# A fused ReGLU layer: w1's first columns by plain load on ScalarE's queue, four plain column blocks, sums moved to GpSimd, rows of x in quarters, a later fit check, another exit

## The chip, the cores and the metric

The kernel runs on one core of one Trainium2 chip. The metric is the time of one execution on the device in microseconds (us), as a median of several executions. A span is the part of it that the profile sees; it is about 1.8 us shorter than the time. All executions told of here were of the fast state.

## The reference

```python
# x: 16 x 256 x 512, w1: 512 x 4096, w2: 2048 x 512, all float32
def reference(x, w1, w2):
    h = x @ w1
    gate, value = np.split(h, 2, axis=-1)
    h = np.maximum(gate, 0) * value
    return (h @ w2).astype(np.float32)
```

## The kernel before

The 4096 rows of x are worked through in four sets of 1024. Each set has a first layer (16 blocks of 128 hidden columns) and a second layer. Both multiply 2x2 blocks of half matrices in float16 by seven products instead of eight (Winograd's form of Strassen's algorithm, P1 to P7). For this, sums S1 to S4 of the left operand and T1 to T4 of the right one must be made. The second layer of one set is interleaved with the first layer of the next.

```python
SUMS = (("S1", "A21", "A22", ADD), ("S2", "S1", "A11", SUB), ("S4", "A12", "S2", SUB), ("S3", "A11", "A21", SUB))
TURNS = (("T1", "B12", "B11", SUB), ("T2", "B22", "T1", SUB), ("T3", "B22", "B12", SUB), ("T4", "B21", "T2", SUB))

def g_sum(eng, go, n, h0, h1):      # a sum of the hidden values g, for the second layer
    for m, i0, i1, op in SUMS:
        if m == n:
            eng.tensor_tensor(go[n][:, h0:h1], go[i0][:, h0:h1], go[i1][:, h0:h1], op=op)
```

At the very start nothing is summed yet, so the first NPLAIN = 2 blocks are computed plainly. The first columns of w1 come by GpSimd's loads, which turn float32 into float16 on their way:

```python
for b in (0, 2):
    nc.sync.dma_start(out=xf[:, b:b + 2], in_=x_v[0, :, b:b + 2])
fetch_w1(0, 0)                      # nc.gpsimd.dma_start into a float16 tile
make_identity(nc, ident[F32])
fetch_w1(0, 1)
# ... (the other loads; two plain blocks; VectorE makes the weight sums of blocks 2 and 3)
```

At the end of the first set's first layer VectorE makes all sums of g and the sum T4 of w2, while GpSimd has made T1 to T3 earlier:

```python
if s == 0:
    for m in ("S1", "S2", "S4", "S3"):
        for h in (0, NHC // 2):
            g_sum(nc.vector, go, m, h, h + NHC // 2)
    w2_op(nc.vector, "T4", 2)
```

A tile of output rows b of the upper half is `o1`, of the lower half `o2`. All lie in four buffers of one name. In the order of use o1(0), o1(1), o1(2), o2(0), o2(1), the fifth needs the buffer of the first, whose store must have landed:

```python
d["o1"] = tmp.tile([P, DO], F32, name="o", tag="o", bufs=4)     # P2
# ...
nc.sync.dma_start(out=out_v[s, 0, b], in_=d["o1"])              # P3
# ...
d["o2"] = tmp.tile([P, DO], F32, name="o", tag="o", bufs=4)     # P7
```

ScalarE sums squares of x, w1 and w2, to see at run time whether their scale suits the float16 way. The rows of x for that come from DRAM, half a set at a time, into one buffer (`xn`). In the last set VectorE judges the sums, TensorE counts across partitions, and VectorE writes a flag. A branch on the flag runs a general way where the scale does not fit (it does fit here):

```python
BESIDE[NS - 1, 3] = [judge]         # and, in it, count at step 5, flag at step 8
BESIDE[NS - 1, 14] = [...]          # the flag is read
# ...
with tc.If(unfit > 0):
    general_way(...)
```

Of the kernel before, what the change touches and what calls it, by code (L numbers as in the profile page):

```python
# [17 lines left out]
TH = 512  # L18
PERIOD = 7
NWARM = 7  # L20
NFILL = 8
NPLAIN = 2
HIGH, LOW = 512.0, 32.0
GS = 2.0 ** -19
SLOT = {"P1": 0, "P5": 1, "P2": 3, "P6": 4, "P3": 5, "P7": 9, "P4": 13}
# [4 lines left out]
@with_exitstack  # L30
def kernel(ctx: ExitStack, tc: tile.TileContext, x, w1, w2, out):






    nc = tc.nc
    x2 = x.flatten_outer_dims()
    out2 = out.flatten_outer_dims()  # L40
    flagpool = ctx.enter_context(tc.tile_pool(name="flagpool", bufs=1))
    flag = flagpool.tile([1, 1], dt.int32, name="flag")
    with ExitStack() as fast:
        unfit = fast_way(fast, tc, x2, w1, w2, out2, flag)
    with tc.If(unfit > 0):
        with ExitStack() as general:
            general_way(general, tc, x2, w1, w2, out2)

# [51 lines left out]
def fast_way(ctx, tc, x2, w1, w2, out2, flag):  # L100
# [23 lines left out]
    x_v = x2.rearrange("(s b p) d -> s p b d", p=P, b=2 * NB)  # L124
    out_v = out2.rearrange("(s h b p) n -> s h b p n", p=P, b=NB, h=2)

    CHUNKS = ((0, 2), (2, 2), (4, 4), (8, 4), (12, 4))
    place = {jb + i: (c, i) for c, (jb, n) in enumerate(CHUNKS) for i in range(n)}
    wr = [wpool.tile([P, 4, 2, n * P], F16, name=f"wr{c}") for c, (_, n) in enumerate(CHUNKS)]
    wt = [wpool.tile([P, 4, 2, n * P], F16, name=f"wt{c}") for c, (_, n) in enumerate(CHUNKS)]  # L130
# [112 lines left out]
    class Plain:  # L243
        def __init__(self, g, jb):
            self.g, self.jb = g, jb

        def open(self):
            self.X = psx.tile([P, TH], F32, name="X", tag="X")
            self.W = psw.tile([P, TH], F32, name="W", tag="W")

        def mm(self, side, a, q):
            ts = slice(q * 256, q * 256 + 256)
            ps = (self.X, self.W)[side]
            for e in range(4):
                name = (("B11", "B21"), ("B12", "B22"))[side][e // 2]
                nc.tensor.matmul(ps[:, ts], W(name, self.jb)[:, e % 2], a[:, e, ts], start=e == 0, stop=e == 3,  # L256
                                 skip_group_check=True)
# [18 lines left out]
    def mm2_stream(s, go):  # L276
# [14 lines left out]
        def step(name, b):  # L291
# [18 lines left out]
            elif name == "P3":  # L310
                yield from mm("P3", b, d["W"], False)
                nc.vector.scalar_tensor_tensor(out=d["o1"][:, HALF:], in0=d["W"], scalar=1 / GS, in1=d["pu"][:, 1],  # L312
                                               op0=MULT, op1=ADD)
                nc.sync.dma_start(out=out_v[s, 0, b], in_=d["o1"])
            elif name == "P7":
                yield from mm("P7", b, d["Y"], False)
                d["o2"] = tmp.tile([P, DO], F32, name="o", tag="o", bufs=4)
                nc.vector.scalar_tensor_tensor(out=d["o2"][:, HALF:], in0=d["Y"], scalar=1 / GS, in1=d["pu"][:, 0],
                                               op0=MULT, op1=ADD)
                if last and b == NB - 1:  # L320
                    nc.sync.dma_start(out=out_v[s, 1, b, :, HALF:], in_=d["o2"][:, HALF:])
            else:
                yield from mm("P4", b, d["Y"], False)
                if last and b == NB - 1:
                    m = HALF // 2
                    nc.scalar.activation(d["o2"][:, :m], d["Y"][:, :m], COPY, scale=1 / GS)
                    nc.scalar.dma_start(out=out_v[s, 1, b, :, :m], in_=d["o2"][:, :m])
                    nc.vector.tensor_scalar(out=d["o2"][:, m:HALF], in0=d["Y"][:, m:], scalar1=1 / GS, scalar2=None,
                                            op0=MULT)
                    nc.sync.dma_start(out=out_v[s, 1, b, :, m:HALF], in_=d["o2"][:, m:HALF])  # L330
                else:
                    nc.scalar.activation(d["o2"][:, :HALF], d["Y"], COPY, scale=1 / GS)
                    nc.sync.dma_start(out=out_v[s, 1, b], in_=d["o2"])
# [33 lines left out]
    g, go = g_tiles()  # L367
    xf = go["S1"].rearrange("p a t -> p (a t)").bitcast(F32).rearrange("p (b d) -> p b d", b=NB)
    xh = go["S2"][:, :NB]

    def turn_first(o, h, b0):
        if h == 0:
            for b in (b0, b0 + 1):
                ps = psy.tile([P, 4, P], F32, name="Y", tag="Y")
                for e in range(4):
                    nc.tensor.transpose(ps[:, e], xf[:, b, e * P:(e + 1) * P], ident[F32])
                copy = nc.scalar.copy if b % 2 else nc.vector.tensor_copy
                copy(out=o["A1"][:, :, b * P:(b + 1) * P], in_=ps)
            return
        ps = psx.tile([P, 4, 2, P], F16, name="X", tag="X")  # L380
        for b in range(2):
            for e in range(4):
                nc.tensor.transpose(ps[:, e, b], xh[:, b0 + b, e * P:(e + 1) * P], ident[F16])
        nc.vector.tensor_copy(out=o["A2"][:, :, b0 * P:(b0 + 2) * P], in_=ps.rearrange("p e b t -> p e (b t)"))

    for b in (0, 2):
        nc.sync.dma_start(out=xf[:, b:b + 2], in_=x_v[0, :, b:b + 2])
    fetch_w1(0, 0)
    make_identity(nc, ident[F32])
    fetch_w1(0, 1)  # L390
    for b in (0, 2):
        nc.gpsimd.dma_start(out=xh[:, b:b + 2], in_=x_v[0, :, NB + b:NB + b + 2])
    make_identity(nc, ident[F16])
    for c in range(1, len(CHUNKS)):
        for g_ in range(2):
            fetch_w1(c, g_)

    xo = x_tiles()
    plain = [Plain(g, jb) for jb in range(NPLAIN)]

    def plain_mm(h, q):
        for side in range(2):
            for p in plain:
                p.mm(side, xo[f"A{h + 1}"], q)

    idle(NWARM)
    turn_first(xo, 0, 0)
    idle(NFILL)
    for p in plain:
        p.open()  # L410
    for p in plain:
        p.mm(0, xo["A1"], 0)
    turn_first(xo, 0, 2)
    for p in plain:
        p.mm(1, xo["A1"], 0)
    idle(3)
    plain_mm(0, 1)
    for p in plain:
        p.close(0)
    turn_first(xo, 1, 0)  # L420
    for p in plain:
        p.open()
    plain_mm(1, 0)
    turn_first(xo, 1, 2)
    plain_mm(1, 1)
    sums = list(SUMS)

    def x_sum(o):
        n, i0, i1, op = sums.pop(0)
        nc.vector.tensor_tensor(o[n], o[i0], o[i1], op=op)  # L430

    x_sum(xo)
    plain[0].close(1)
    x_sum(xo)
    w1_first = [t for t in TURNS]

    def w1_one():
        m, a, b, o = w1_first.pop(0)
        nc.vector.tensor_tensor(W(m, 2, 2), W(a, 2, 2), W(b, 2, 2), op=o)  # L439

    w1_one()
    plain[1].close(1)
    w1_one()
    x_sum(xo)
    w1_one()
    x_sum(xo)
    w1_one()

    def look_x(s, i):
        b = i // 2 % NB  # L450
        t = xn if s else (xf, xh)[i // 2 // NB]
        look(t[:, b, i % 2 * 256:i % 2 * 256 + 256], 4 * NB * s + i, 256)

    def look_w1(i):
        c, o = place[i // 2 * 2]
# [2 lines left out]
    def look_w2(i):  # L458
        look(w2_sb[:, 2 * i:2 * i + 2].rearrange("p h n -> p (h n)"), NW + i, 1024)

    def fetch_rows(s, h):
        t = xpool.tile([P, NB, D], F16, name="xn")
        nc.sync.dma_start(out=t, in_=x16[s][h * TH:(h + 1) * TH].rearrange("(b p) d -> p b d", p=P))
        return t

    def judge():
        n = st.shape[1]
# [4 lines left out]
        nc.vector.memset(fit, 1.0)  # L472
        with nc.allow_low_precision("whole numbers below 2048"):
            nc.vector.tensor_reduce(out=fit[:, :1], in_=ok, axis=mybir.AxisListType.X, op=ADD)
        BESIDE[NS - 1, 5] = [lambda: count(fit, P * n)]

    def count(fit, n):
        ps = psw.tile([P, TH], F32, name="W", tag="W")
        nc.tensor.matmul(ps[:1, :1], fit[:, :1], fit[:, 1:], start=True, stop=True)
        BESIDE[NS - 1, 8] = [lambda: nc.vector.tensor_scalar(out=flag, in0=ps[:1, :1], scalar1=n - 0.5, scalar2=None,  # L480
                                                             op0=LT)]

    LOOKS = {}

    for s in range(NS):
        for i in range(4 * NB):
            LOOKS[s, min(i + 2, NJ - 1) if s == 0 else i] = [lambda s=s, i=i: look_x(s, i)] + (
                LOOKS.get((s, NJ - 1), []) if s == 0 and i > NJ - 3 else [])
    for s in range(NS - 1):
        for i in range(8):  # L490
            f = (lambda i=i + 8 * s: look_w1(i)) if s < 2 else (lambda i=i: look_w2(i))
            BESIDE[s, 7 + 2 * i] = [f]
    BESIDE[NS - 1, 3] = [judge]
    verdict = []
    BESIDE[NS - 1, 14] = [lambda: verdict.append(nc.values_load(
        flag[0:1, 0:1], min_val=0, max_val=1, skip_runtime_bounds_check_because="a comparison wrote it"))]

    prev = None
# [2 lines left out]
    for s in range(NS):  # L501
# [21 lines left out]
        for at in range(first * PERIOD, last + PERIOD):  # L523
            if at in plan:
                jb, n = plan[at]
                if n == "P1" and s and jb == 4:
                    late = fetch_rows(s, 1)
                if n == "P1" and s and jb == 8:
                    xn = late
                getattr(blocks[jb], n)()  # L530
                if n == "P5":
                    for f in LOOKS.get((s, jb), ()):
# [9 lines left out]
            else:  # L542
                advance(prev, 4)
        if s == 0:
            for m in ("S1", "S2", "S4", "S3"):
                for h in (0, NHC // 2):
                    g_sum(nc.vector, go, m, h, h + NHC // 2)
            w2_op(nc.vector, "T4", 2)
        else:
            for m in ("S1", "S2", "S4"):  # L550
                g_sum(nc.vector, go, m, NHC - BY_DVE, NHC)
# [1 line left out]
        if s + 1 < NS:  # L553
            xo = x_tiles()
            for h in range(2):
                for k in range(2):
                    nc.sync.dma_start_transpose(out=xo[f"A{h + 1}{k + 1}"],
                                                in_=x16[s + 1][h * TH:(h + 1) * TH, k * 256:k * 256 + 256])
            xn = fetch_rows(s + 1, 0)
            advance(stream, 100)  # L560
            sums = list(SUMS)
            for _ in SUMS:
                x_sum(xo)
            if s == 0:
                w1_ops(nc.vector, 0, 2)
            advance(stream, MM2 - TAIL - 100 - done)
        else:
            advance(stream, MM2)
# [30 lines left out]
```

## Time and profile before

| | before |
|---|---|
| time, median of 3 | 332.25 us (330.86 to 333.29) |
| span of the profiled execution | 332.0 us (that execution took 333.9) |
| TensorE busy | 93% of the span |
| mean granted clock in it | 0.984 |
| idle time of TensorE from 8.5 to 33.7 us | 8.2 us |
| the first second layer: VectorE's first sum of g to the first product of set 1 | 23.86 us |
| last product to end of span | 5.76 us |

In a waits view each line is: engine, tile and line that waited, "<-" what it waited for, then us in total, number of waits, longest. In a timeline each line is: start, length, engine, line, operation, output "<-" inputs, shapes, number of instructions, and in brackets the idle time before them and what ended it. The lines of before are in the prediction.

### The profile page before, as it was taken

The page shows a single profiled execution, that of the slowest core. Times are in us where ns is not written, and L with a number is a line of the kernel's source. Part 1 is how long each engine was busy: PE and PEld are TensorE (multiplying, and loading weights), DVE is VectorE, ACT ScalarE, POOL GpSimd, SP SyncE. Part 2 cuts the span into 40 slices and gives each one's busy share as a digit, 9 for nine tenths or more (in the row PEclk, how much of TensorE's full clock was granted, in tenths as well). Part 3 has the DMA queues.
Part 4 walks back from the last instruction along what each step waited for, and adds up shares of the span by engine and source line. Part 5 has one row for each costly group of instructions (what it writes and reads, how often), then busy time and mean ns, then how long its engine had stood idle before and what let it go on. Part 6 is the DMA issues. An engine that isn't in the chain of part 4 may idle for free.

```text
span 332.0 us, 5158 instructions
## 1 busy us (share of the span) xinstructions
PE 309.3 (93%) x1879; PEld 184.7 (56%) x1879; DVE 217.8 (66%) x338; ACT 187.5 (56%) x449; POOL 144.3 (43%) x128
## 2 busy tenths in 40 slices
PE   8756999999799999999999999999999999997993
PEld 4632444457684443448884443458884443455882
DVE  1369888879835887886526887885527887885211
ACT  2214667657457665655856766665856666752230
POOL 8359999800001334994001334993001434993000
PEclk9998999999999999999999999999999999998997
DMA  8999996036311010017311010017321020000113
GB/s 192 200 207 207 200 198 131 0 65 126 126 65 63 3 32 31 1 21 167 133 69 61 0 52 13 0 33 148 141 89 38 2 63 0 1 2 0 65 67 131
DMA packets 29390, 26.07 MB, mean 79 GB/s; under 512 B 13648, under 2 KB 24784, under 8 KB 29264
## 3 DMA queue, kind: packets, MB, share of 16 engines
q0 software_dynamic: 8080, 9.96, 17.7%
q1 hardware_dynamic: 21136, 15.67, 15.8%
q8 instruction: 16, 0.26, 0.3%
q14 instruction: 14, 0.11, 0.1%
q10 hardware_dynamic: 144, 0.07, 0.1%
HBM read 24.12 MB, written 11.53 MB: 107 GB/s over the span
## 4 chain that ended last, share of the span: by engine, by line
PE 81%; DVE 11%; ACT 2%; issue 2%; DMA 2%; DVEq 0%; ACTq 0%
PE Y L203 22%; PE X L203 14%; PE W L203 14%; PE Y L283 11%; PE W L283 8%; PE X L283 6%; DVE g_S L272 3%; PE Y L175 2%; DVE x_S L430 1%; DVE wt L439 1%; DVE cc L230 1%; DMA xn<-x 1%; PE X L256 1%; DVE g L240 1%; DVE cc L236 1%
## 5 line engine op out<-in xcount | busy, mean ns | idle before, releaser
L272 POOL TENSOR_TENSOR g_S<-g 128x512 f16<-128x512 f16 x42 | 48.5, 1154 | 144.0 <-DVE g L240 144.0
L203 PEld LDWEIGHTS <-wt 128*128 128x128 f16 x496 | 48.3, 98 | 68.3 <-issue 9.8
L203 PE MATMUL Y<-x_S,wt 128*128 128x512 f16 x248 | 74.2, 381 | 1.1 <-DVE x_S L430 1.0
L203 PE MATMUL X<-x_A,wr 128*128 128x512 f16 x248 | 74.1, 380 | 0.0
L230 DVE SCALAR_TENSOR_TENSOR cc<-W,pu 128x512 f32<-128x512 f32 x62 | 42.8, 691 | 39.4 <-ACT pu L224 36.4
L203 PEld LDWEIGHTS <-wr 128*128 128x128 f16 x372 | 36.3, 98 | 43.5 <-issue 2.6
L210 ACT COPY Y<-X 128x512 f32<-128x512 f32 x62 | 35.4, 571 | 42.0 <-PE X L203 26.9
L283 PEld LDWEIGHTS <-g_S 128*128 128x128 f16 x512 | 50.4, 99 | 7.9 <-DVE g_S L272 1.6
L224 ACT ACTIVATE pu<-Y 128x512 f32<-128x512 f32 x62 | 36.9, 596 | 15.7 <-PE Y L203 15.7
L231 DVE SCALAR_TENSOR_TENSOR g<-X,cc 128x512 f16<-128x512 f32 x62 | 42.9, 691 | 2.4
L240 DVE SCALAR_TENSOR_TENSOR g<-Y,cc 128x512 f16<-128x512 f32 x62 | 42.2, 681 | 2.8 <-PE Y L203 2.8
L283 PEld LDWEIGHTS <-g 128*128 128x128 f16 x384 | 37.8, 99 | 10.5 <-issue 2.0
L236 DVE SCALAR_TENSOR_TENSOR cc<-Y,pu 128x512 f32<-128x512 f32 x62 | 42.2, 681 | 0.3
L203 PE MATMUL Y<-x_A,wt 128*128 128x512 f16 x124 | 36.7, 377 | 4.0 <-DVE cc L236 4.0
L203 PE MATMUL W<-x_S,wt 128*128 128x512 f16 x124 | 37.2, 382 | 3.1 <-DVE wt L439 3.1
L217 ACT ACTIVATE pu<-W 128x512 f32<-128x512 f32 x62 | 37.4, 602 | 3.3 <-PE W L203 3.3
L203 PE MATMUL W<-x_S,wr 128*128 128x512 f16 x124 | 37.1, 381 | 0.3 <-DVE x_S L430 0.3
L283 PE MATMUL X<-w_sb,g 128*128 128x256 f16 x256 | 32.2, 277 | 0.0
L312 DVE SCALAR_TENSOR_TENSOR o<-W,pv 128x256 f32<-128x256 f32 x16 | 6.7, 423 | 38.1 <-PE W L283 38.0
L283 PE MATMUL Y<-v_T,g_S 128*128 128x256 f16 x256 | 30.9, 273 | 0.4 <-DVE g_S L272 0.4
L191 ACT ACTIVATE sq<-xn 128x256 f16<-128x256 f16 x48 | 19.9, 415 | 4.0 <-DMA xn<-x 4.0
L272 POOL TENSOR_TENSOR g_S<-g_S,g 128x512 f16<-128x512 f16 x18 | 20.8, 1156 | 1.4
(68 smaller groups left out, 293.3 us busy)
## 6 DMA issues: line engine op xcount, KB each, us to landing
out_dram<-o SPq DMA_DIRECT2D x31, 256.0 KB, 2.0
wr<-in_w_dram POOLq DMA_DIRECT2D x6, 512.0 KB, 14.6
x<-in_x_dram POOLq DMA_DIRECT2D x3, 1024.0 KB, 13.0
xn<-x SPq DMA_DIRECT2D x6, 512.0 KB, 4.0
w_sb<-in_w_dram POOLq DMA_DIRECT2D x4, 512.0 KB, 8.2
g_S<-in_x_dram SPq DMA_DIRECT2D x2, 512.0 KB, 3.8
wr<-in_w_dram POOLq DMA_DIRECT2D x4, 256.0 KB, 7.5
g_S<-in_x_dram POOLq DMA_DIRECT2D x2, 256.0 KB, 7.7
```

Source lines behind the costliest of these rows:

```text
L191: nc.scalar.activation(sq, t, SQUARE, scale=(P / of) ** 0.5, accum_out=st[:, at:at + 1])
L203: nc.tensor.matmul(ps, W(wn, self.jb)[:, b], self.xo[xn][:, b, :], start=fresh and b == 0, stop=b == 1, skip_group_check=True)
L210: nc.scalar.copy(out=self.Y, in_=self.X)
L217: nc.scalar.activation(self.p5, self.W, COPY, scale=GS)
L224: nc.scalar.activation(self.u2, self.Y, COPY, scale=GS)
L230: nc.vector.scalar_tensor_tensor(out=self.c12, in0=self.W, scalar=GS, in1=self.u2, op0=MULT, op1=ADD)
L231: nc.vector.scalar_tensor_tensor(out=self.g[:, self.jb, :TH], in0=self.X, scalar=0.0, in1=self.c12, op0=MAX, op1=MULT)
L236: nc.vector.scalar_tensor_tensor(out=self.c22, in0=self.Y, scalar=GS, in1=self.p5, op0=MULT, op1=ADD)
L240: nc.vector.scalar_tensor_tensor(out=self.g[:, self.jb, TH:], in0=self.Y, scalar=0.0, in1=self.c22, op0=MAX, op1=MULT)
L272: eng.tensor_tensor(go[n][:, h0:h1], go[i0][:, h0:h1], go[i1][:, h0:h1], op=op)
L283: nc.tensor.matmul(ps, go[gn][:, k, b * P:(b + 1) * P], V[vn][:, k, :], start=fresh and k == 0, stop=k == NHC - 1, skip_group_check=True)
L312: nc.vector.scalar_tensor_tensor(out=d["o1"][:, HALF:], in0=d["W"], scalar=1 / GS, in1=d["pu"][:, 1], op0=MULT, op1=ADD)
```

## The change

It means to start the products earlier, to take S3 and T4 off VectorE in the first second layer, and to remove three smaller waits. Cut to its core (left out: w1's next columns come in smaller loads, fewer filler products run at the start, and VectorE makes the weight sums of blocks 2 and 3 in the first second layer, as those blocks are now plain in the first set):

```diff
-NPLAIN = 2
+NPLAIN = 4
...
-    with tc.If(unfit > 0):
+    with tc.If(unfit > 0, preferred_fallthrough_block=False):
...
+    wl = g[:, NJ - 4:]...bitcast(F32)...          # float32 landing place for w1's first columns
+    def cast_w(g_):
+        nc.scalar.copy(out=wr[0][:, :2, g_], in_=wl[:, :2, g_])
+        nc.vector.tensor_copy(out=wr[0][:, 2:, g_], in_=wl[:, 2:, g_])
-    fetch_w1(0, 0)
+    for g_ in range(2):
+        nc.scalar.dma_start(out=wl[:, :, g_], in_=w1_v[:, :, g_, :2 * P])
...
+                if n == "P1" and s == 0 and jb in (10, 12, 14):
+                    g_sum(nc.gpsimd, go, "S3", jb - 10, jb - 8)
         if s == 0:
-            for m in ("S1", "S2", "S4", "S3"):
+            g_sum(nc.gpsimd, go, "S3", 6, 8)
+            w2_op(nc.gpsimd, "T4")
+            for m in ("S1", "S2", "S4"):
                 for h in (0, NHC // 2):
                     g_sum(nc.vector, go, m, h, h + NHC // 2)
-            w2_op(nc.vector, "T4", 2)
...
-        t = xpool.tile([P, NB, D], F16, name="xn")               # rows of x: halves, one buffer
+        rows[s, q] = xpool.tile([P, 2, D], F16, name=f"xn{q % 2}")   # quarters, two buffers
...
-    BESIDE[NS - 1, 3] = [judge]     # count 5, flag 8, read 14
+    BESIDE[NS - 1, 6] = [judge]     # count 12, flag 14, read 18
...
-   nc.vector.tensor_scalar(out=d["o2"][:, m:HALF], ...)          # the last half tile
+   o3 = tmp.tile([P, DO], F32, name="o", tag="o", bufs=4)[:, :m]
```

## The prediction

> **What bounds the kernel now.** I read the page's shares first, then the chain, then the waits of TensorE, then busy times by stage.
>
> ```profile
> PE 81%; DVE 11%; ACT 2%; issue 2%; DMA 2%; DVEq 0%; ACTq 0%
> ```
>
> TensorE holds 81% of the chain that ended last and is busy 93% of 332.0 us: a gain can only come from TensorE's idle time, cold time and filler. The waits of TensorE (for whom: total us, times, longest) name it:
>
> ```profile
> PE Y L203 <- DVE cc L236: 4.0, 5, 1.3
> PE W L203 <- DVE wt L439: 3.1, 1, 3.1
> PE X L256 <- DVE x_A L384: 2.5, 2, 1.7
> PE W L479 <- DVE fit L474: 2.1, 1, 2.1
> PE Y L283 <- DVE o L318: 1.7, 2, 0.9
> ```
>
> L203 are the seven-product ("Winograd") blocks of the first layer, L256 its plain blocks, L283 the second layer, L479 the fit check. Busy times by stretch (length, then busy us of PE, PEld, DVE, ACT, POOL, then granted clock) place them:
>
> ```profile
> 8.50:33.70 25.20, 17.02 (x116) 10.74 (x115) 16.50 (x19) 6.91 (x15) 16.35 (x16) 0.93 1.26 203
> 33.70:70.00 36.30, 36.30 (x169) 16.29 (x168) 30.46 (x48) 25.00 (x62) 31.22 (x19) 1.00 0.63 119
> 70.00:98.60 28.60, 25.63 (x222) 21.32 (x221) 20.68 (x31) 15.49 (x37) 0.00 (x0) 1.00 0.42 111
> 301.90:308.80 6.90, 4.75 (x29) 3.49 (x28) 2.27 (x8) 1.15 (x3) 0.00 (x0) 0.75 0.00 0
> ```
>
> Four places lose time: the start (8.2 of 25.2 us idle, and a stretch at half clock), the first second layer (3.0 us), the fit check (2.2 us, clock 0.75), and 0.70 us once in each of sets 1 to 3, where ScalarE waits for rows of x. Elsewhere TensorE is full.
>
> **What the Trainium skill says.** (1) "TensorE: Matmul & The Clock Gate", Part 1: the array runs at half clock after an idle window of about 3.4 us and regains full clock after as long a busy one. The trace agrees on the price, not on the threshold: after idle times of only 3.05 us (24.4) and 2.15 us (304.2) the granted clock was 0.51 for 3.4 us, costing about 1.7 us each. (2) "SBUF — State Buffer", Who interferes with whom: a VectorE instruction with two SBUF inputs and a GpSimd one that reads SBUF exclude each other for whole instructions. The trace agrees:
>
> ```profile
> 22.44 1.60 POOL L158 TENSOR_TENSOR wt<-wr 128x512 f16<-128x512 f16 x1
> 22.95 1.37 DVE L439 TENSOR_TENSOR wt<-wr 128x512 f16<-128x512 f16 x1
> 300.32 1.15 POOL L272 TENSOR_TENSOR g_S<-g,g_S 128x512 f16<-128x512 f16 x1
> 300.65 1.37 DVE L272 TENSOR_TENSOR g_S<-g 128x1024 f16<-128x1024 f16 x1
> ```
>
> The VectorE sum of 22.95 takes 0.42 us when GpSimd rests (at 90.7), here 1.37, ending 0.28 us after GpSimd's 24.04; at 300.65 likewise. They alternate. (3) "DMA: Bandwidth & Descriptors", Issuing engines are not separate DMA queues: all queues share the same 16 DMA engines. I use it below; at the start the x rows on SyncE's queue move at about 400 KB/us, and GpSimd's casting loads read about as fast once alone (512 KB each 1.25 to 1.4 us). (4) "Runtime: NRT & Kernel Launch", Instruction fetch mechanics: a taken branch out of the fetched window stalls. Seen: VectorE branches at 326.65 and goes on at 329.89.
>
> **The change part by part.**
>
> *Start.* GpSimd's first w1 loads land at 8.04 and 9.69 although issued at 1.26 and 2.73; their first packet moves at about 4.5, while SyncE's x rows (issued 0.74, 1.27) move from 2.0 and land at 4.06 and 5.48. The change brings those w1 columns as float32 on ScalarE's queue and casts them on ScalarE and VectorE. Now 2 MB share the engines from 2.0: at 400 KB/us, with GpSimd's packets taking part of it after 4.6, gate columns land at about 6 to 7 and value columns at about 9.3. Both casts stand ahead of the x copies in VectorE's and ScalarE's order, so first plain matmuls at about 8.3 (before 8.5), the W half at about 10.4 (before 10.41). No gain yet. From there, before: two plain blocks, then two Winograd blocks, whose weight sums (8 VectorE instructions against GpSimd's) starve TensorE: idle 1.72, 0.78, 3.05, 0.28, 1.03, 1.31 us and half clock. Block 4 starts at 33.72, with two products of block 3 outstanding. After: four plain blocks need 4 x 16 matmuls of 512 columns at 0.2155 us = 13.8 us against 13.8 - 4 x 0.2155 = 12.9 for two and two; the price is 0.9 us. 0.9 us of it is done at 10.4; add 0.9 for the transposes of x's second half and 0.4 for one copy: block 4 starts at about 24.7, its weights made by GpSimd from about 16 to 21. Filling the pipeline costs about 0.9 us (an extra evacuation on ScalarE); the two outstanding products save 0.86. **Gain about 9 us.** The squares for the fit check no longer pile up at block 15 (three in a row at 69.3): another 0.7. VectorE's sums of g, at 74.75 before, can thus start at about 65.1.
>
> *First second layer.* The S3 sum (2 x 1.18 us) and T4 (2 x 0.68) leave VectorE for GpSimd, where S3 is 4 instructions at 2.13 (as wt 128x1024) and T4 one at 4.08 (as v_T 128x2048). Before, GpSimd was done at 65.26 and VectorE began long after:
>
> ```profile
> 61.18 4.08 POOL L165 TENSOR_TENSOR v_T<-w_sb 128x2048 f16<-128x2048 f16 x1
> 74.75 2.35 DVE L272 TENSOR_TENSOR g_S<-g 128x2048 f16<-128x2048 f16 x2
> ```
>
> After, GpSimd starts 4 us earlier (its w1 chunk is half as large) and ends v_T at about 61.2, then has 12.6 us more: to 73.8. VectorE starts at 65.1, 8 us inside it. By the alternation, S1's halves are done at 66.7 and 70.0 (one S3 between), S2's at 73.3 and, after T4, 78.6, S4's at 79.8 and 81.0. TensorE wants S1 at 67.2 and works 1.75 us on each sum: it stalls about 2.4 us in S1 and 2 and 4.8 us in S2, with half clock behind. This stage then ends some 21 us after VectorE's start instead of 14.4: **6.5 us given back**. 9.7 - 6.5 leaves 3.2 us. A smaller gain at the start means less overlap, so the two offset each other.
>
> *x rows in quarters.* Now one buffer holds half of the rows, so its refill can be issued only after the eighth square and the ninth waits for it:
>
> ```profile
>   ACT sq L191: 4.0, 3
> ```
>
> (who waited for the xn loads). Each ends in a TensorE wait of 0.70 us (129.68, 203.86, 278.01). With two quarter buffers the refill has four blocks, 12 us, against a landing time of 4.0. **Gain 2.1 us.**
>
> *Late fit check.* TensorE no longer stands still for the reduction (2.15 us and the 0.16 us matmul at 304.22); it has 28 matmuls, then S1, S2, S4, ready at 302.0, 302.7, 303.5 when wanted at 302.8, 304.5, 306.3. The count comes six steps later, when its operand is old. No idle time, no half clock: 304.31 - 302.0 = 2.3, plus 1.7. **Gain 4.0 us.**
>
> *Exit.* The last half tile gets its own buffer: VectorE's last copy (326.64, held by ScalarE's) starts 0.3 us earlier, but ScalarE's own store lands at 329.98 against 330.15, so 0.17. The fall-through only moves the far jump behind the short branch: SyncE must make it after the last landing, about 0.4 us as its jump at 327.39 to 327.84. **Loss 0.2 us.**
>
> Sum: 3.2 + 2.1 + 4.0 - 0.2 = 9.1 us; 332.25 - 9.1 = 323.1. I go to 322.5, because what is unsure in the contention lies mostly on the good side.
>
> **The rivals.** *A: no contention in the first second layer.* GpSimd may finish sooner, or may not hold long instructions' lock throughout: no run shows a 4 us one against VectorE. Then the sums cost nothing, S3 and T4 off VectorE save another 3.6 us, and the time is about 313. Against it: the alternation is plain for 1.15 us instructions. *B: the loads are the bound at the start.* 1 KB rows of float32 may move worse than 2 KB rows; if the value columns land at 11.5, block 4 starts at 27, overlap falls with it, and the time is about 323 to 325. *C: ScalarE becomes the bound at the start* (casts, four evacuations, squares): it has some 1.2 us per 1.72 us of plain half block, so I expect nothing beyond what is counted; if wrong, 1 to 2 us. *D: a gap over 2 us anywhere in the plain blocks* brings half clock: 1.7 us more.
>
> **Range and chances.** A bad start with a bad contention gives 326.5, half of the contention absent 316.5 to 318. The 2% line is 325.6, 6.65 us below. The fit check and the quarters alone bring 6.1, almost certain, so faster by over 2% needs only 0.6 us net from the start: 0.78. Slower by over 2% would take 16 us of new loss: 0.01.
>
> **What would show it.** Block 4's first product near 24.7; TensorE waits for L387-type copies and weight sums gone at the start; in the first second layer VectorE's g_S instructions stretched beyond 1.2 us beside GpSimd's g_S and v_T, TensorE waits of 2 to 5 us on g_S, clock below 1 there; no ScalarE wait for xn; no wait for fit and clock 1.00 at 302 to 309; SyncE's jump after the last landing. I am wrong if the g_S waits are absent (A), or if the first W matmul starts well after 10.4 (B).

## The result, and the profile after

The changed kernel took 327.88 us in the median of 4 executions (327.47 to 328.63) against 332.77 us for the kernel before; the ratio is 0.9865 with a 95% interval of 0.9817 to 0.9913. A ratio here is the mean time of one kernel's fast executions over that of the other's of the same rounds, so it is not quite the ratio of the medians. The gain is clear of zero but, by the whole interval, under 2%. The prediction was 322.5 us with a range of 316.5 to 326.5, and "faster by over 2%" at 0.78. It was wrong: the gain is 4.5 us of the 9.1 that its sum promised.

The busy times by stretch of the changed kernel, with the same columns as before's (start and end, length, then busy us of PE, PEld, DVE, ACT, POOL, then granted clock, DMA share, GB/s):

```profile
8.50:33.70 25.20, 24.36 (x148) 14.08 (x147) 15.81 (x22) 13.99 (x33) 19.43 (x19) 1.00 1.30 205
60.00:98.60 38.60, 30.90 (x244) 24.27 (x243) 28.17 (x34) 18.27 (x44) 17.12 (x6) 0.91 0.33 89
301.90:308.80 6.90, 5.39 (x49) 4.49 (x48) 1.75 (x5) 0.56 (x3) 0.00 (x0) 1.00 0.32 116
```

The start is now nearly full (24.36 of 25.20 us, at full clock from 9.67 on; before 17.02). The first second layer is not: 7.7 us idle, mean clock 0.91. The stretch of the fit check has full clock, but TensorE still stands for 1.5 us. The waits of TensorE say why:

```profile
PE Y L285 <- DVE g_S L274: 6.0, 2, 4.4
PE W L285 <- DVE g_S L274: 1.7, 1, 1.7
PE Y L285 <- DVE flag L488: 1.5, 1, 1.5
PE Y L175 <- DVE warm L169: 1.5, 1, 1.5
PE Y L285 <- DVE o L320: 0.7, 1, 0.7
```

All waits of before's list that the change aimed at are gone. In their place stand waits on the sums of g (7.7 us), one behind the flag, and one for an output tile (the wait on "warm" is the first 1.46 us of the span, ahead of everything). The timeline of the changed kernel in the first second layer, of GpSimd, VectorE and TensorE in turn:

```profile
61.81 10.32 POOL L274 TENSOR_TENSOR g_S<-g 128x1024 f16<-128x1024 f16 x4
72.10 5.03 POOL L165 TENSOR_TENSOR v_T<-w_sb,v_T 128x2048 f16<-128x2048 f16 x1
...
65.62 4.53 DVE L274 TENSOR_TENSOR g_S<-g 128x2048 f16<-128x2048 f16 x2
70.08 8.13 DVE L274 TENSOR_TENSOR g_S<-g_S,g 128x2048 f16<-128x2048 f16 x2
78.13 2.35 DVE L274 TENSOR_TENSOR g_S<-g,g_S 128x2048 f16<-128x2048 f16 x2
...
70.21 1.48 PE L285 MATMUL W<-v_T,g_S 128*128 128x256 f16 x12 [1.74 <-DVE g_S L274]
73.28 0.61 PE L285 MATMUL Y<-v_T,g_S 128*128 128x256 f16 x4 [1.58 <-DVE g_S L274]
78.26 2.74 PE L285 MATMUL Y<-v_T,g_S 128*128 128x256 f16 x12 [4.38 <-DVE g_S L274]
```

Two VectorE instructions of the same size take 2.35 us where GpSimd rests (78.13) and 8.13 us across GpSimd's T4. TensorE stands three times, the last time for 4.38 us, and the trace has the clock at half from 74.53 to 81.35. The 40-slice line of the page shows it:

```profile
PEclk9999999995999999999999999999999999999998
```

And the new wait near 307 us, VectorE first, then TensorE:

```profile
307.13 0.42 DVE L320 SCALAR_TENSOR_TENSOR o<-Y,pv 128x256 f32<-128x256 f32 x1 [2.32 <-DMA out_dram<-o]
307.48 0.14 DVE L488 TENSOR_SCALAR flag<-W 1x1 int32<-1x1 f32 x1
...
307.61 1.03 PE L285 MATMUL Y<-v_T,g 128*128 128x256 f16 x8 [1.51 <-DVE flag L488]
```

TensorE is said to wait for the flag, but the flag only stands last in a queue. VectorE waited 2.32 us for a store to land, because o2(1) needs the buffer of o1(0).

The traces of all kernels can be cut at the same four marks. This ledger (worked out from the start times of instructions and the end of the last product, in us) is used below:

| kernel | to VectorE's first sum of g | to first product of set 1 | to last block of set 3 | to last product | to end of span |
|---|---|---|---|---|---|
| before | 74.75 | 23.86 | 195.01 | 32.62 | 5.76 |
| changed | 65.62 | 30.30 | 192.82 | 30.38 | 6.49 |
| changed, once more (after_again) | 66.03 | 30.39 | 193.24 | 30.11 | 5.98 |
| e1_sums_back | 65.48 | 23.88 | 192.57 | 30.77 | 6.35 |
| e2_split | 65.55 | 28.53 | 192.90 | 28.72 | 6.19 |
| e3_own | 65.48 | 30.88 | 192.81 | 28.71 | 6.21 |
| e4_exit | 65.60 | 31.53 | 192.69 | 28.71 | 5.39 |
| t4_back | 66.28 | 26.36 | 193.91 | 30.02 | 5.99 |
| start_only | 65.47 | 23.85 | 196.59 | 32.63 | 5.57 |
| start_spare | 65.80 | 22.76 | 194.99 | 32.64 | 5.41 |
| b_offload | 73.67 | 25.84 | 195.21 | 32.63 | 5.24 |
| b_late | 73.44 | 23.88 | 195.05 | 28.74 | 5.18 |
| b_quarters | 74.02 | 23.85 | 191.82 | 31.08 | 5.94 |
| after_spare | 65.57 | 31.71 | 191.79 | 28.71 | 6.33 |
| best2 | 65.83 | 22.18 | 192.01 | 28.72 | 5.44 |
| best3 | 64.53 | 22.18 | 192.00 | 28.71 | 5.69 |

The second column of the changed kernel and of those with the same sums (after_again, e3_own, e4_exit, after_spare) reads 30.30 to 31.71. All five have 6.83 us of half clock there, but at different times: from 74.53 in the changed kernel, where TensorE stood for 3.7 us of it, and from 77.13 in after_spare, where it stood for 1.3. So differences of this size in that column need not be the work of the edits.

### The profile page after: what moved, and what is told of

The parts are those of the page before. It is cut to its first block, busy times and chain, and to the rows that moved or that the text cites. A ratio compares the mean times of both kernels' runs of the same rounds, so it can differ in the third digit from the quotient of the medians.

```text
span 325.6 us, 5158 instructions
## 1 busy us (share of the span) xinstructions
PE 306.3 (94%) x1868; PEld 183.7 (56%) x1868; DVE 216.9 (67%) x331; ACT 189.0 (58%) x450; POOL 160.3 (49%) x133
## 5 line engine op out<-in xcount | busy, mean ns | idle before, releaser
L274 POOL TENSOR_TENSOR g_S<-g 128x512 f16<-128x512 f16 (+1 forms) x46 | 58.8, 1281 | 127.0 <-DVE g L240 125.1
L203 PEld LDWEIGHTS <-wt 128*128 128x128 f16 x480 | 46.8, 97 | 56.2 <-issue 2.5
L203 PE MATMUL X<-x_A,wr 128*128 128x512 f16 x240 | 71.3, 378 | 0.2 <-ACT Y L210 0.2
L203 PE MATMUL Y<-x_S,wt 128*128 128x512 f16 x240 | 71.4, 379 | 0.0
L285 PEld LDWEIGHTS <-g 128*128 128x128 f16 x384 | 37.5, 98 | 10.9 <-issue 2.7
L231 DVE SCALAR_TENSOR_TENSOR g<-X,cc 128x512 f16<-128x512 f32 x60 | 41.5, 691 | 2.3
L240 DVE SCALAR_TENSOR_TENSOR g<-Y,cc 128x512 f16<-128x512 f32 x60 | 40.9, 681 | 2.8 <-PE Y L203 2.8
L236 DVE SCALAR_TENSOR_TENSOR cc<-Y,pu 128x512 f32<-128x512 f32 x60 | 40.9, 681 | 0.1
L203 PE MATMUL W<-x_S,wt 128*128 128x512 f16 x120 | 35.7, 379 | 0.0
L203 PE MATMUL W<-x_S,wr 128*128 128x512 f16 x120 | 35.7, 379 | 0.0
L274 POOL TENSOR_TENSOR g_S<-g,g_S 128x512 f16<-128x512 f16 x18 | 21.8, 1213 | 1.4
```

The costliest lines, as they stand in the source:

```text
L203: nc.tensor.matmul(ps, W(wn, self.jb)[:, b], self.xo[xn][:, b, :], start=fresh and b == 0, stop=b == 1, skip_group_check=True)
L231: nc.vector.scalar_tensor_tensor(out=self.g[:, self.jb, :TH], in0=self.X, scalar=0.0, in1=self.c12, op0=MAX, op1=MULT)
L236: nc.vector.scalar_tensor_tensor(out=self.c22, in0=self.Y, scalar=GS, in1=self.p5, op0=MULT, op1=ADD)
L240: nc.vector.scalar_tensor_tensor(out=self.g[:, self.jb, TH:], in0=self.Y, scalar=0.0, in1=self.c22, op0=MAX, op1=MULT)
L285: nc.tensor.matmul(ps, go[gn][:, k, b * P:(b + 1) * P], V[vn][:, k, :], start=fresh and k == 0, stop=k == NHC - 1, skip_group_check=True)
```

## The experiments

Fourteen runs were made, all with correct results, each of five rounds against the kernel before on the same chip (four groups of runs, on four chips). Where a ratio r is told as a gain in us, it is (1 - r) x 332.1, the mean of the 44 executions of the kernel before that these four groups of runs had.

**Is the shared port the cause? e1_sums_back**: S3 and T4 go back to VectorE.

```diff
-                if n == "P1" and s == 0 and jb in (10, 12, 14):
-                    g_sum(nc.gpsimd, go, "S3", jb - 10, jb - 8)
-            g_sum(nc.gpsimd, go, "S3", 6, 8)
-            w2_op(nc.gpsimd, "T4")
-            for m in ("S1", "S2", "S4"):
+            for m in ("S1", "S2", "S4", "S3"):
...
+            w2_op(nc.vector, "T4", 2)
```

> The changed kernel with S3 and T4 of the first second layer back on VectorE, as before. Theory (the shared SBUF port costs the stage 6 to 7 us and brings the half clock): VectorE's sums of g run at 1.2 us each, TensorE's waits on g_S fall from 7.7 us to about 1, no half clock there, the stage ends 14.4 instead of 20.7 us after VectorE's start; time 6 us below the changed kernel, about 321.5 to 322.5 us. Rival (the stage is bound by something else, as the evacuations or the missing g of block 15): within 1.5 us of the changed kernel.

It took 320.84 us, ratio 0.9646 (0.9618 to 0.9675): a gain of 11.8 us where the changed kernel has 4.5. Its timeline has VectorE's sums at 1.2 us each:

```profile
65.48 2.35 DVE L274 TENSOR_TENSOR g_S<-g 128x2048 f16<-128x2048 f16 x2
67.75 2.35 DVE L274 TENSOR_TENSOR g_S<-g_S,g 128x2048 f16<-128x2048 f16 x2
70.02 2.35 DVE L274 TENSOR_TENSOR g_S<-g,g_S 128x2048 f16<-128x2048 f16 x2
```

TensorE's waits on g_S are two of 0.35 us, there is no half clock, and the stage takes 23.88 us instead of 30.30. VectorE has more work than in the changed kernel and TensorE gets it sooner. The theory holds and its rival falls.

**Whole instructions, or shared bandwidth? e2_split**: the same work on GpSimd in smaller pieces.

```diff
-                    g_sum(nc.gpsimd, go, "S3", jb - 10, jb - 8)
+                    g_sum(nc.gpsimd, go, "S3", jb - 10, jb - 9)
+                    g_sum(nc.gpsimd, go, "S3", jb - 9, jb - 8)
...
-            w2_op(nc.gpsimd, "T4")
+            w2_op(nc.gpsimd, "T4", 4)
```

> The changed kernel with GpSimd's S3 cut into 8 instructions and T4 into 4, each about 1.05 us. Theory (the two engines exclude each other for whole instructions and alternate one for one): VectorE's six sums take about 2.25 us each, the 4.4 us wait of TensorE becomes about 1.7, the stage ends 1.5 to 3.5 us sooner, time 324 to 326.5 us. Rival (they share bandwidth, so the cut does not matter, or GpSimd keeps the port through a row of instructions): same as the changed kernel within 0.7 us.

It took 325.67 us, ratio 0.9809 (0.9782 to 0.9836). VectorE and GpSimd in its timeline:

```profile
65.55 4.02 DVE L274 TENSOR_TENSOR g_S<-g 128x2048 f16<-128x2048 f16 x2
69.49 4.26 DVE L274 TENSOR_TENSOR g_S<-g_S,g 128x2048 f16<-128x2048 f16 x2
73.67 4.26 DVE L274 TENSOR_TENSOR g_S<-g,g_S 128x2048 f16<-128x2048 f16 x2
...
61.90 12.86 POOL L274 TENSOR_TENSOR g_S<-g 128x512 f16<-128x512 f16 x8
```

Each VectorE sum now takes about 2.1 us: its own 1.18 plus one GpSimd instruction of about 1. The 4.4 us wait became waits of at most 1.5 us, and the stage is 1.8 us shorter than in the changed kernel. Instruction by instruction, GpSimd's end at 66.39, 68.48, 70.58, 72.67, 74.76 and 76.85, and VectorE's between them at 67.47, 69.56, 71.66, 73.75, 75.84 and 77.93: the engines take turns, one for one. In bytes nothing changed, so shared bandwidth cannot explain it. The time alone would not show this: its interval touches the changed kernel's, and the trace of this run also lacks the wait near 307 (last stretch 28.72 us instead of 30.38).

**Which of the two sums? t4_back**: T4 alone back on VectorE.

```diff
-            w2_op(nc.gpsimd, "T4")
...
+            w2_op(nc.vector, "T4", 2)
```

> The changed kernel with T4 alone back on VectorE, S3 left on GpSimd. Theory (the long T4 is what holds S2's second half for 4.4 us and brings the half clock, S3 costs the two waits before it): TensorE's waits on g_S are 3 to 3.5 us in sum, none over 2, no half clock there, time about 5 us below the changed kernel, near 323. Rival (S3 and T4 cost alike, by their length, 8.5 to 4.1 us): about 2.5 us below, near 325.5.

It took 323.95 us, ratio 0.9734 (0.9691 to 0.9778), a gain of 8.8 us: 4.3 of the 7.3 us between the changed kernel and e1_sums_back come from T4, 3.0 from S3. The sums beside S3 alone:

```profile
66.28 4.28 DVE L274 TENSOR_TENSOR g_S<-g 128x2048 f16<-128x2048 f16 x2
70.48 4.27 DVE L274 TENSOR_TENSOR g_S<-g_S,g 128x2048 f16<-128x2048 f16 x2
74.67 2.35 DVE L274 TENSOR_TENSOR g_S<-g,g_S 128x2048 f16<-128x2048 f16 x2
```

TensorE's waits on g_S are 1.49, 1.58 and 0.52 us. The expectation said no half clock; the profiled execution, the slowest of the six, had one stretch of 3.41 us of it. The size lies near the theory (4.2 us under the changed kernel by the medians of the same group of runs, 4.7 by their means; expected 5, rival 2.5).

**Does the move cost this with the old start too? b_offload**: S3 and T4 on GpSimd in the kernel before. The edit is that part of the change alone.

> The kernel before with S3 and T4 of the first second layer on GpSimd, and nothing else changed. Theory (the price is set by how far GpSimd's row reaches into VectorE's sums: with the old start VectorE begins at 74.75 and GpSimd ends near 78): VectorE's first sum waits for T4 until about 78, one TensorE wait of about 2 to 3 us on g_S, the two waits of 0.7 and 0.95 behind S3 and T4 gone: within 1.5 us of the kernel before, about 331 to 334. Rival (the move costs 6 to 7 us wherever the start lies): 338 to 339.

It took 333.24 us, ratio 1.0033 (0.9993 to 1.0073): a loss of 1.1 us. In its timeline GpSimd, VectorE and TensorE:

```profile
73.60 4.05 POOL L165 TENSOR_TENSOR v_T<-w_sb,v_T 128x2048 f16<-128x2048 f16 x1
...
73.67 6.21 DVE L272 TENSOR_TENSOR g_S<-g 128x2048 f16<-128x2048 f16 x2
...
78.80 0.61 PE L283 MATMUL W<-v_T,g_S 128*128 128x256 f16 x4 [2.72 <-DVE g_S L272]
```

VectorE asks 0.07 us after GpSimd has begun T4, waits for all of it, and is then free. In the ledger the stage is 2.0 us longer than in b_late. The same move costs 1.1 us with the old start and 7.3 with the new one. What it costs is the overlap, and the change itself made the overlap, by letting VectorE begin 8 us sooner (65.62 against 73.67) while GpSimd came to S3 only 3.5 us sooner (61.81 against 65.26).

**The start alone: start_only.** The changed kernel with the edits of e1_sums_back, and with rows in halves, early fit check and old exit.

> The kernel before with the new start alone (plain w1 loads on ScalarE's queue and four plain blocks; the last half tile also keeps its own buffer; S3 and T4 on VectorE, rows in halves, early fit check and exit as before). Theory (the start itself gains 9 us, and only S3 and T4 on GpSimd gave it back): first product of block 4 near 25.7, VectorE's first sum of g near 65.5, the first second layer without waits over 1 us, time 9 us under the kernel before, about 323. Rival (part of the start's gain is lost later whatever the sums do, as VectorE now also makes the weight sums of blocks 2 and 3 in the first second layer): gain 6 us or less.

It took 325.76 us, ratio 0.9814 (0.9776 to 0.9851): a gain of 6.2 us, not 9. VectorE's first sum of g is where it was expected (65.47), and the stage is as long as before (23.85). So the rival's reason falls, although its size, 6 us or less, was nearly met. The ledger shows a loss in the stretch after it: 196.59 instead of 195.01 us. The trace has one new wait there; VectorE, then TensorE:

```profile
151.45 0.43 DVE L320 SCALAR_TENSOR_TENSOR o<-Y,pv 128x256 f32<-128x256 f32 x1 [0.39 <-PE Y L285]
154.01 0.42 DVE L320 SCALAR_TENSOR_TENSOR o<-Y,pv 128x256 f32<-128x256 f32 x1 [2.13 <-DMA out_dram<-o]
...
154.49 1.03 PE L285 MATMUL Y<-v_T,g 128*128 128x256 f16 x8 [1.32 <-DVE o L320]
```

It is the wait of 307 us again, in another set. The store was issued at 150.22 and landed at 153.89, 3.67 us later; most stores of this size land after 2.0. In this trace a single packet of 16 KB on the queue for instructions ran from 151.47 to 152.40. The store's other packets were done by about 153.0, and then a trickle followed at 0.07 of the engines' capacity, that is one of 16. In the changed kernel the late store of 302.95 (landed after 4.06 us) likewise has such a packet from 303.87 to 305.49. In the kernel before, the packet of that part of the program ran from 310.92 to 312.09, before its stores' data moved, and they landed after 2.02 us. So a fetch of instructions that falls on a store seems to delay one sixteenth of it. I did not move a fetch on purpose; this rests on coincidence in time, though on much of it. Over all 16 traces (stores of output tiles, up to 6 us before the last product), 47 stores had such a packet start between 0.5 us before their issue and 1.5 us after it, and 46 of these landed after 2.6 to 4.3 us; of the 384 others 377 landed within 2.5 us.

**Is that wait the missing part? start_spare and after_spare.** The second output tile of each set goes into an unused half of its evacuation tile, so that it needs no landed store. start_spare is start_only with it, after_spare the changed kernel with it.

```diff
-                d["pu"] = tmp.tile([P, 2, TH], F32, name="pv", tag="tmp")[:, :, :HALF]
+                both = tmp.tile([P, 2, TH], F32, name="pv", tag="tmp")
+                d["pu"], d["spare"] = both[:, :, :HALF], both[:, :, HALF:]
...
-                d["o2"] = tmp.tile([P, DO], F32, name="o", tag="o", bufs=4)
+                if b == 1:
+                    d["left"], right = d["spare"][:, 0], d["spare"][:, 1]
+                else:
+                    d["o2"] = ...       # as before
```

> start_only with one difference: the second output tile of each set's second layer lies in the unused half of its evacuation tile and so waits for no store. Theory (1.5 us of the start's gain is given back near 153, where the store of the first output tile lands 3.7 instead of 2.0 us after its issue and VectorE, then TensorE, stands behind it): TensorE's wait there is gone in the profile, time 1.0 to 1.5 us below start_only's ratio of 0.981, so about 0.977, or 324.4 us. Rival (the wait moves to the next user of a buffer, or comes from another cause): ratio as start_only's.

> The changed kernel with that same difference alone. Theory: the waits of 0.7 to 1.2 us near 159 and of 1.2 to 1.5 us behind the flag near 307 are both gone, nothing else moves: ratio 0.979 to 0.981 against 0.987 of the changed kernel, about 325.5 us. Rival (the waits show only in the profiled executions): ratio 0.985 or more.

start_spare took 322.24 us, ratio 0.971 (0.9678 to 0.9742), 3.5 us better than start_only by the ratios. Its trace accounts for 2.7: the stretch to the last block of set 3 is back at 194.99 us, and the first second layer is 1.1 shorter, since there too o2(1) waited for a store, as it did in the kernel before (0.9 us at 87.2). So 1.6 us were given back by a wait that the new start called up, and 1.1 were there all along. after_spare took 325.79 us, ratio 0.9812 (0.9783 to 0.9842), expected 0.979 to 0.981; both its waits are gone. In its ledger the two late stretches are 1.0 and 1.7 us shorter than the changed kernel's; the first second layer is 1.4 us longer, by where the half clock fell.

**The flag or the store? e3_own**: the second output tile of the last set alone gets another buffer (an idle tile for rows of x).

```diff
-                d["o2"] = tmp.tile([P, DO], F32, name="o", tag="o", bufs=4)
+                if last and b == 1:
+                    spare = xpool.tile([P, 2, D], F16, name="xn0")
+                    d["o2"] = spare.rearrange("p a d -> p (a d)").bitcast(F32)
+                else:
+                    d["o2"] = tmp.tile([P, DO], F32, name="o", tag="o", bufs=4)
```

> The changed kernel with a buffer of its own for the second output tile of the last set, so that VectorE need not wait for the store of the first one. Theory (the new TensorE wait of 1.5 us near 307 comes from VectorE waiting for that store, the flag only stands behind it): VectorE's wait on the output and TensorE's wait behind the flag are gone in the profile, time 1.0 to 1.5 us below the changed kernel in those executions in which the store lands late. Rival (the flag or the fit check's own order holds TensorE): the wait of 1.5 us stays.

It took 326.82 us, ratio 0.984 (0.9816 to 0.9864). The flag instruction is where it was in the program, yet no wait behind it is left, although the first store again landed late, after 4.33 us. VectorE, then TensorE:

```profile
305.70 0.42 DVE L324 SCALAR_TENSOR_TENSOR xn<-Y,pv 128x256 f32<-128x256 f32 x1 [0.45 <-PE Y L285]
306.04 0.14 DVE L492 TENSOR_SCALAR flag<-W 1x1 int32<-1x1 f32 x1
...
305.50 1.91 PE L285 MATMUL Y<-v_T,g 128*128 128x256 f16 x16
```

The last stretch is 28.71 instead of 30.38 us. The profiled instruction named "flag" was not the cause. The times (0.8 us by the ratios, with overlapping intervals) would not have shown it; the trace does.

**The late fit check alone: b_late.** The four step numbers of the change, in the kernel before.

> The kernel before with the late fit check alone. Prediction's step: 4.0 us (2.3 of waits, 1.7 of half clock). Theory now: the two waits go, but VectorE may stand behind the store of the first output tile, for 0 to 1.5 us: gain 2.5 to 4 us, about 328.5 to 330. Rival (the fit check's half clock does not count, or the gain is only what the changed kernel showed in that stretch): 2.2 us.

It took 328.71 us, ratio 0.9911 (0.9873 to 0.9949): a gain of 3.0 us. The stretch from the last block of set 3 to the last product is 28.74 us. With the early check it is 32.62 in the profile of before, which had half clock there, and 31.08 in that of b_quarters, which had the wait of 2.3 us without half clock. So the wait is worth 2.3 us (each of the five traces with the early check has it, at 2.15 us or more of idle time), and the half clock 1.5 more in some executions.

**Rows in quarters alone: b_quarters.**

> The kernel before with rows of x in quarters alone. Prediction's step: three TensorE waits of 0.70 us behind ScalarE's late rows go, gain 2.1 us, about 330.2. Rival (the waits only change their name, and the evacuations hold TensorE anyway): under 1 us.

It took 328.75 us, ratio 0.9901 (0.9861 to 0.9941): a gain of 3.3 us, more than either theory; the interval (2.0 to 4.6 us) still holds the 2.1, so the trace has to decide. The timeline of before, of TensorE at the first of the three waits:

```profile
128.38 0.59 PE L203 MATMUL W<-x_S,wr 128*128 128x512 f16 x2
129.68 0.59 PE L203 MATMUL Y<-x_A,wt 128*128 128x512 f16 x2 [0.70 <-DVE cc L236]
```

Two matmuls make a product, and products follow each other at 0.43 us when nothing waits. Here it took 1.30 us from start to start, so this stall cost 0.87, not 0.70. The idle time shown is too small by 0.16 us, as each matmul is recorded with 0.38 us but the next one starts 0.2155 after it. Another 0.2 us was lost in small delays of the same block: the step from one block's first product to the next is 3.04 us in the mean, and 4.10 to 4.15 where such a wait is (read off b_late, which has the same waits). Three times 1.08 is the 3.2 us that the ledger shows (195.01 to 191.82).

**The exit alone: e4_exit.** The branch of before in the changed kernel.

> The changed kernel with the branch of before at its exit. Theory (SyncE's far jump of 0.5 us stands on the path after the last store has landed): SyncE jumps while the stores are under way, the span ends about 1.85 instead of 2.35 us after the last landing, time 0.5 us lower. Rival (the end waits for other engines' jumps, or for the runtime): no difference.

It took 326.72 us, ratio 0.984 (0.9811 to 0.987); the interval holds the changed kernel's ratio, so the times do not settle it. The trace does: its last store landed at 322.08 and the span ended at 323.93, 1.85 us later, against 323.25 and 325.62, 2.37 us, in the changed kernel. SyncE's far jump of 0.5 us stands on the path there. The other traces agree: from the last landing to the end of the span it is 2.36 to 2.38 us in the seven with the new exit and 1.72 to 1.99 us in the nine with the old one.

**The yardstick: after_again**, the changed kernel once more.

> The changed kernel itself once more, as the yardstick of this call. Expected near 327.9 us. Theory (half clock behind the 4.4 us wait is there in every execution, while the half clock windows of the kernel before come and go): its executions spread less than those of the kernel before, and its granted clock never reaches 0.995.

It took 328.12 us (327.61 to 329.32), ratio 0.9884 (0.9846 to 0.9921). Its granted clock was 0.978 to 0.988 in six executions, and these spread by 1.7 us against 3.3 of the kernel before in the same group, both as expected. The kernel before, in its 44 executions, had 0.980 to 1.000: the 11 with 0.995 or more have a mean span of 329.4 us, the 15 with 0.985 or less 331.2. The profiled execution of before, at 0.984 and 332.0, is among the longest (the longest of the 44 has a span of 332.1).

The clock records of the traces give a reason. "TensorE: Matmul & The Clock Gate", Part 1 of the Trainium skill, says that activity is watched in a window of 3413 ns that runs freely and does not start with the kernel. The traces agree: in all of them, each stretch at one clock between the first rise and the end is a whole number of 3.41 us (1, 2, 5, 19, 71, 81 ...), on a grid whose offset differs from execution to execution (first rise between 4.2 and 10.9 us). An idle gap of 2.15 us brings half clock when it falls into one window, as at 302.07 in the profile of before, and none when a boundary splits it: in b_quarters the 2.3 us gap at 298.11 had 1.81 of them in one window and passed at full clock. That this is what spreads the 44 executions is argued, since they have no clock records; but their mean clocks lie near 1.000, 0.995, 0.990, 0.985 and 0.980, and 3.41 us at half clock in a span of 330 take off 0.005.

**Better than both: best2 and best3.** best2 is the changed kernel with S3 and the second half of T4 on VectorE, the first half of T4 on GpSimd (which rests from 62 to 65), the old exit and the edit of after_spare. best3 also copies the second pair of x blocks before it casts w1's value columns:

```diff
-    cast_w(1)
     turn_pair(xo, 2)
+    cast_w(1)
     for p in plain[:2]:
+        p.mm(0, xo["A1"], 1)
+    for p in plain[:2]:
         p.open_w()
         p.mm(1, xo["A1"], 0)
...
```

> A version that should beat both: the changed kernel with S3 and the second half of T4 on VectorE, the first half of T4 on GpSimd where it is idle, the exit of before, and the second output tile of each set in the unused half of its evacuation tile, so that it waits for no store. Theory: the e1_sums_back time of 320.6 less 0.5 for the exit, 0.6 to 1.9 for the flag and store waits, 0.7 for T4: about 317.5 us. Rival (the store waits only move): 319.5.

> As best2, with the copies of the second pair of x blocks ahead of the cast of the value columns, and the matmuls that need them ahead of those that need the value columns, so that TensorE does not stand for 1.6 us near 9.7. Theory: first product of block 4 at 24.3 instead of 25.7, time 1.0 to 1.5 us below best2, about 316.3. Rival (the weights of block 4 or the loads of x's second half then bind): same as best2.

best2 took 316.00 us, ratio 0.9525 (0.9487 to 0.9563); best3 took 314.74 us, ratio 0.9473 (0.9438 to 0.9507), 17.4 us under the kernel before by the medians (332.14). Both came out under what was expected (317.5 and 316.3). Block 4's first product is at 25.95 in best2 and at 24.66 in best3, so the new order of the start is worth 1.3 us. The waits on g_S that best3 has left:

```profile
PE W L285 <- DVE g_S L274: 0.3, 1, 0.3
PE Y L285 <- DVE g_S L274: 0.3, 1, 0.3
```

Its granted clock was 0.996 to 1.000, and its six executions lie within 0.6 us: with no gap near 2 us, there is no half clock to come and go.

## Why the prediction was wrong

The terms, each measured alone by ratio:

| term | predicted gain, us | measured, us | by |
|---|---|---|---|
| start | 9.7 | 6.2 | start_only |
| given back in the first second layer | -6.5 | -7.3 | changed kernel against e1_sums_back (0.9865, 0.9646) |
| rows in quarters | 2.1 | 3.3 | b_quarters |
| late fit check | 4.0 | 3.0 | b_late |
| exit | -0.2 | -0.5 | e4_exit, by the trace |
| sum | 9.1 | 4.7 | 4.5 measured for the change (3.9 in the repeat) |

The terms add up, but with an interval of some 1.2 us either way on each ratio the agreement to 0.2 us is partly luck. It also hides two effects of under 2 us: the terms leave out the wait near 307 (1.7 us in the ledger), and the start's term holds 1.6 us of a store's wait that came to only 1.0 us in the changed kernel. Point by point:

- **The contention was foreseen rightly.** The step said stalls of about 2.4, 2 and 4.8 us, half clock behind, and a stage that ends 21 us after VectorE's start. The trace has 1.74, 1.58 and 4.38 us, half clock from 74.53, and 20.7 us (86.31 - 65.62). It gives back 6.4 us in the trace, 7.3 by times. Rival A fell. The choice of 322.5 instead of 323.1, because the contention's doubt lay "mostly on the good side", went the wrong way.
- **The step that failed is the size of the start**: "Gain about 9 us" and "another 0.7". The mechanism was right: block 4's first product came at 25.75 (predicted 24.7) and VectorE's first sum at 65.62 (predicted 65.1). But the gain was taken from one profiled execution and subtracted from a median of others. That execution had VectorE's first sum at 74.75; with the same start, b_late, b_offload and b_quarters have it at 73.44 to 74.02. Of these b_late and b_offload had no half clock at the start; the prediction counted it as lost in every execution. That is 0.7 to 1.3 us of the missing 3.5. In start_only the first sum came at 65.47 instead of 65.1, which is 0.4. Another 1.6 us were given back at 153, where o2(1) waited for a late store (start_only against start_spare). About 0.2 to 0.8 us of the term stays unexplained, within the interval of start_only's ratio (1.2 us either way).
- **The margin was misjudged with it.** "Faster by over 2% needs only 0.6 us net from the start" is the sentence that set 0.78. The net of start and contention was predicted as 3.2 us; it was about -1.1 (6.2 - 7.3). The move of S3 and T4 ate the whole new start. The 0.6 us also left out the exit's loss of 0.2. That the quarters and the fit check alone would bring 6.1 us (6.3 measured) came true by luck: one was too small by 1.2 us and the other too large by 1.0.
- **The quarters** were undersized. The price of each wait was read from the idle time (0.70 us); the step from block to block shows 1.08.
- **The late fit check** was oversized. The 2.3 us of wait were right; the 1.7 us of half clock were counted as certain, and the clock grid grants them to some executions only. "No idle time, no half clock" was right on the clock, wrong on the idle time: in the changed kernel TensorE stood 1.51 us behind the flag. The step had not looked at the four output buffers. In before's profile VectorE already waited 1.6 us so in the first second layer, and in the last set the store landed 0.1 us before the buffer was wanted (313.96, 314.08): there was no room left.
- **The exit** had the right cause and half the size: 0.52 us more after the last landing. The 0.17 us from the last tile's own buffer did not come: VectorE's last copy still waited 1.68 us, ended by ScalarE's. The gap from last product to last landing was 4.13 us instead of 3.91.
- **Rival B** took part: the value columns landed at 10.16 instead of 9.3, and the first W product came at 11.43 instead of 10.4, 1 us late. best3 shows that this second was to be had by another order: 1.3 us. Rivals C and D did not show: TensorE's waits on ScalarE at the start are 0.5 us in all, and after the first W product no idle time there is over 0.3 us.

## What to carry to other kernels

Before you move work to GpSimd, lay its whole row of instructions in time beside VectorE's, as it will be after the other parts of the change: a stage that starts sooner can run into work that was harmless before. Cut what must run beside VectorE into instructions no longer than the other engine can afford to wait; here that won back 1.8 us of the stage's 6.4, and moving the work back won it all. Price a stall from start to start of the products around it, take a profile of a median execution (or several) as the base of a sum, and look for buffers whose reuse hangs on a store with no time to spare.

## What the Trainium skill lacked or had wrong

- "TensorE: Matmul & The Clock Gate", Part 1, puts the fall to half clock after an idle window of about 3.4 us and warns of gaps longer than that (it also says that frequent short idle times can bring it, without a size). Here 1.87 to 1.95 us of idle time within one window were enough (t4_back, e2_split), while windows with 1.93 (e3_own, e4_exit) and 1.96 us (b_late) passed: a window a little under half busy is already the limit, and a gap of 2.15 us can cost 1.5 us.
- "SBUF — State Buffer", Who interferes with whom, says that whoever issues first holds the shared port for the whole instruction and that issue order decides who blocks; what happens when both have rows of instructions waiting it does not say. Then the two engines alternated one for one here: VectorE's sums of 1.18 us took about 2.1 beside GpSimd's of about 1 us (e2_split), and GpSimd's four of S3 took 10.32 us instead of 8.4 (changed kernel against b_offload).
- "Runtime: NRT & Kernel Launch", Instruction fetch mechanics, calls the cost of crossing a 16 KiB block mostly hidden. For the engine that fetches that may hold; what it does to other transfers the page does not say. Here a 16 KB packet of 0.9 to 1.7 us that fell on a store of 256 KB went with a landing after 2.6 to 4.4 us instead of 2.0, and with up to 1.9 us of waiting of TensorE where a buffer hung on that store (e1_sums_back; 1.5 in the changed kernel).
